# Weight sums of a seven-product matrix multiply, formed by accumulating DMAs in place of VectorE subtractions

## The chip, the core and the metric

The kernel runs on one NeuronCore of one Trainium2 chip. The core has five engines that each work through their own queue in order: TensorE (PE, with PEld for its weight loads), VectorE (DVE), ScalarE (ACT), GpSimd (POOL) and SyncE (SP, which here only issues DMAs). Data moves between the chip's main memory and the on-chip memory (128 partitions) by DMAs, which run on 16 DMA engines. The metric is the device time of one execution in microseconds; lower is better.

## The reference

One layer of a hybrid decoder on a sequence of 512 tokens with model width 2048. One large input projection feeds two branches, an mLSTM and a latent attention; their gated outputs are summed and projected back.

```
h = rms_norm(x, norm_g)                       # (512, 2048)
proj = h @ w_in                               # (2048, 15440), split into
(q_a, k_a, v_a, o_a, i_a, f_a, z_a, c_q, c_kv, k_r, z_b, g_a, g_b) = split(proj)
y_a = (sigmoid(o_a) * rms_norm(mlstm(q_a, k_a, v_a, ...)) * silu(z_a)) @ w_a
y_b = (attention(c_q, c_kv, k_r) * silu(z_b)) @ w_b
out = x + (sigmoid(g_a) * y_a + sigmoid(g_b) * y_b) @ w_out
```

Everything is float32. The five column blocks v_a, o_a, z_a, g_a and g_b of the projection, each 2048 columns wide, are where the change lies.

## The kernel before

TensorE multiplies in a rounded float32 format, so every operand is cut into a rounded high part and a remainder: `split` (L104) casts on ScalarE (L105) and subtracts on VectorE (L106), and each product takes three matmuls, high by high, high by low, low by high.

The five blocks are computed as ten jobs of 1024 columns (`strassen`, called for each of o, z, g_a, g_b, v twice). A job multiplies the 512 x 2048 input by a 2048 x 1024 weight block. Input and weights are cut into 2 x 2 quarters, and seven products of quarters take the place of eight. A weight quarter is 1024 rows by 512 columns; call them Q0 (top left), Q1 (top right), Q2 (bottom left), Q3 (bottom right). The seven passes p = 0 to 6 use these weights:

| pass | 0 | 1 | 2 | 3 | 4 | 5 | 6 |
|---|---|---|---|---|---|---|---|
| before | Q0 | Q1-Q0 | Q3-Q1+Q0 | Q3 | Q3-Q1 | Q2 | Q3-Q1+Q0-Q2 |

Each pass has four steps j, one for 256 rows of the quarter, so a job has 28 steps and the stage 280. In a step a tile of 128 partitions x 2 x 512 floats (512 KB) is split by `part` into `wh` (three buffers) and `wl` (two buffers), and `mult` runs 12 matmuls of 512 columns on it (L506 to L508). The program is written so that the split of step n+1 stands ahead of the matmuls of step n.

`prep` stands two steps ahead. It loads quarter tiles on SyncE's queue and forms the sums on VectorE (`minus`, L462). Per job and j it holds a tile x that starts as Q0 and is changed in place for passes 1, 2 and 6, and three tiles of a ring for Q1, Q3 and Q2; pass 4 changes the tile of Q3 in place. So a job has 16 loads of 512 KB and 16 subtractions. Outputs of passes are combined by `finish`, which puts small pieces of work on a list (`later`); one piece is taken per step. Results are stored by DMAs on ScalarE's queue, eight of 256 KB per job (16 for the two jobs of v).

The order in each engine's queue is set by the framework's scheduler from the program's order and from when buffers come free; it puts in the semaphore waits. GpSimd has no work between the input normalisation and the last steps of the stage. The program is built with `dynamic_dma_scratch_size=1024`, the bytes of each partition reserved for lists of DMAs that GpSimd's software issues; the kernel before issues none.

Of the kernel before, what the change touches and what calls it, by code (L numbers as in the profile page):

```python
# [11 lines left out]
F32 = mybir.dt.float32  # L12
# [4 lines left out]
ALU = mybir.AluOpType  # L17
AX = mybir.AxisListType

P = 128  # L20
# [14 lines left out]
OFF_C, OFF_ZB, OFF_GA, OFF_GB = 8208, 9296, 11344, 13392  # L35

NB_RAW, NB_W, NB_L, NB_A, NB_B, NB_HEAD, NB_T, NB_ACC, NB_AUX = 4, 3, 2, 15, 12, 17, 6, 5, 3
NB_X, NB_RING, NB_HI, NB_LO = 5, 8, 3, 2

KEYS_AHEAD, ATTN_STEP, MLSTM_STEP, OUT_AHEAD, RELOAD_STEP = 8000, 7800, 6000, 10000, 4000  # L40
EARLY = {"lat", "c", "gz", "vh", "vl", "rope", "rk"}
# [3 lines left out]
def hybrid_kernel(  # L45
# [8 lines left out]
    V, A, G, PE, SP = nc.vector, nc.scalar, nc.gpsimd, nc.tensor, nc.sync  # L54
# [21 lines left out]
    def nm(s):  # L76
        uid[0] += 1
        return f"{s}_{uid[0]}"
# [25 lines left out]
    def split(dst_hi, dst_lo, src):  # L104
        A.copy(dst_hi, src)  # L105
        V.tensor_tensor(dst_lo, src, f32(dst_hi), ALU.subtract)  # L106
# [39 lines left out]
    later = []  # L146
# [67 lines left out]
    H8 = KD // 2  # L214
# [70 lines left out]
    r = const([P, T], F32, "r")  # L285
# [14 lines left out]
    def build(j):  # L300
        f = whole[j]

        def normal():
            V.tensor_tensor(f, f, rB.unsqueeze(1).broadcast_to([P, 2, S]), ALU.mult)

        def parts():
            a = sap.tile([P, 2, 256], F32R, tag=f"a11_{j}", name=nm("a11"))
            b = tmp(512, "a21", F32R).rearrange("p (a c) -> p a c", a=2)
            for dst, n in ((a, 0), (b, 256)):
                split(dst[:, 0, :], dst[:, 1, :], f[:, 0, n:n + 256])  # L310
                SP.dma_start(htop_d[j][:, :, n:n + 256], f32(dst))
            hi = h8p.tile([P, S], F32R, tag=f"h8h{j}", name=nm("h8h"))
            lo = h8p.tile([P, S], F32R, tag=f"h8l{j}", name=nm("h8l"))
            split(hi, lo, f[:, 1, :])
            a11.append(a)
            hN[H8 + j] = (hi, lo)

        sums = []

        def combine():  # L320
            a, b = tmp(512, "s12"), tmp(512, "s34")
            s1, s2, s3, s4 = a[:, 0:256], a[:, 256:512], b[:, 0:256], b[:, 256:512]
            V.tensor_tensor(s1, f[:, 0, 256:512], f[:, 1, 256:512], ALU.add)
            V.tensor_tensor(s3, f[:, 0, 0:256], f[:, 0, 256:512], ALU.subtract)
            V.tensor_tensor(s2, s1, f[:, 0, 0:256], ALU.subtract)
            V.tensor_tensor(s4, f[:, 1, 0:256], s2, ALU.subtract)
            sums.extend((a, b))

        def split_sums():
            hi = sap.tile([P, 4, 256], F32R, tag=f"sh{j}", name=nm("sh"))  # L330
            lo = sap.tile([P, 4, 256], F32R, tag=f"sl{j}", name=nm("sl"))
            for n, src in enumerate(sums):
                src = src.rearrange("p (a c) -> p a c", a=2)
                split(hi[:, 2 * n:2 * n + 2, :], lo[:, 2 * n:2 * n + 2, :], src)
            sh.append(hi)
            sl.append(lo)

        return normal, parts, combine, split_sums
# [101 lines left out]
    def strassen(jobs, comb):  # L440

        count = [0]

        def load(src, row, col, ring):
            if ring:
                q = count[0] % NB_RING
                count[0] += 1
                raw = st["rra" if q < NB_RING - 1 else "rrb"].tile([P, 2, 512], F32, tag=f"rr{q}", name=nm("rr"))
            else:
                raw = st["rx"].tile([P, 2, 512], F32, tag="rx", name=nm("rx"), bufs=NB_X)  # L450
            SP.dma_start(raw, src[row:row + 256, col:col + 512].rearrange("(r p) c -> p r c", p=P))
            return raw

        half = H8 * P

        def prep(c, p, j):
            src, col = c["src"], c["col"]
            x, ring = c["x"], c["ring"]
            row = j * 256

            def minus(dst, a, b):
                V.tensor_tensor(dst, a, b, ALU.subtract)  # L462

            if p == 0:
                x[j] = load(src, row, col, False)
            elif p == 1:
                ring[0, j] = load(src, row, col + 512, True)
                minus(x[j], ring[0, j], x[j])
            elif p == 2:
                ring[1, j] = load(src, half + row, col + 512, True)  # L470
                minus(x[j], ring[1, j], x[j])
            elif p == 4:
                minus(ring[1, j], ring[1, j], ring[0, j])
            elif p == 5:
                ring[2, j] = load(src, half + row, col, True)
            elif p == 6:
                minus(x[j], x[j], ring[2, j])

        def part(c, p, j):
            w = c["ring"][1 if p in (3, 4) else 2, j] if p in (3, 4, 5) else c["x"][j]  # L480
            hi = st["wh"].tile([P, 2, 512], F32R, tag="sthi", name=nm("wh"), bufs=NB_HI)
            lo = st["wl"].tile([P, 2, 512], F32R, tag="stlo", name=nm("wl"), bufs=NB_LO)
            split(hi, lo, w)
            c["w"] = c.get("w", []) + [(hi, lo)]

        def mult(c, p, j):
            ps = c["ps"]
            if j == 0:
                if p == 0:
                    ps["a"] = [acc(), acc()]  # L490
                elif p == 1:
                    ps["c"] = [acc(), acc()]
                elif p in (2, 6):
                    ps["b"] = [aux(), aux()]
                elif p == 4:
                    ps["d"] = [acc(), aux()]
            out = ps["acbcdab"[p]]
            hi, lo = c["w"].pop(0)
            for n in range(2):
                k = 2 * j + n  # L500
                lh, ll = comb(p, k)
                for i in range(2):
                    tok = slice(i * P, (i + 1) * P)
                    first = k == 0 and p not in (3, 5)
                    cont = p in (3, 5)
                    PE.matmul(out[i], lh[:, tok], hi[:, n, :], start=first, stop=False, skip_group_check=cont)  # L506
                    PE.matmul(out[i], lh[:, tok], lo[:, n, :], start=False, stop=False, skip_group_check=cont)  # L507
                    PE.matmul(out[i], ll[:, tok], hi[:, n, :], start=False, stop=k == H8 - 1, skip_group_check=cont)  # L508

        def finish(c, p):  # L510
            ps, outs = c["ps"], c["outs"]

            def keep(name, src):
                c[name] = st["s15"].tile([P, 2, 512], F32, tag=name, name=nm(name))
                later.extend(lambda i=i: A.copy(c[name][:, i, :], src[i]) for i in range(2))

            def summed(i, t, n, a, b, op):
                o = tmp(512, "co")
                V.tensor_tensor(o, a, b, op)
                outs[n](t, o, True)  # L520

            if p == 0:
                keep("s1", ps["a"])
            elif p == 1:
                keep("s5", ps["c"])
            elif p in (2, 4):
                u, src = c["s1"], ps["b" if p == 2 else "d"]
                later.extend(lambda i=i: V.tensor_tensor(u[:, i, :], src[i], u[:, i, :], ALU.add) for i in range(2))
                if p == 4:
                    later.extend(lambda i=i: summed(i, 2 + i, 1, c["s5"][:, i, :], u[:, i, :], ALU.add) for i in range(2))  # L530
            elif p == 3:
                later.extend(lambda i=i: summed(i, i, 1, ps["c"][i], c["s1"][:, i, :], ALU.add) for i in range(2))
            elif p == 5:
                later.extend(lambda i=i: outs[0](i, ps["a"][i], False) for i in range(2))
            else:
                later.extend(lambda i=i: summed(i, 2 + i, 0, c["s1"][:, i, :], ps["b"][i], ALU.subtract) for i in range(2))

        steps = []
        for src, col, outs in jobs:
            c = dict(src=src, col=col, outs=outs, x={}, ring={}, ps={})  # L540
            steps += [(c, p, j) for p in range(7) for j in range(H8 // 2)]
        prep(*steps[0])
        prep(*steps[1])
        part(*steps[0])
        for n, s in enumerate(steps):
            if n + 2 < len(steps):
                prep(*steps[n + 2])
            if n + 1 < len(steps):
                part(*steps[n + 1])
            mult(*s)  # L550
            run_later()
            if s[2] == H8 // 2 - 1:
                finish(s[0], s[1])
            yield 12 * 512
# [13 lines left out]
    st = {n: open_pool(n, "right") for n in STP}  # L568
# [682 lines left out]
```

## Time and profile before

| | |
|---|---|
| median of 3 runs | 2174.47 us (2172.08 to 2177.78) |
| the profiled execution, its own time | 2176.62 us |
| its span, first to last instruction | 2174.9 us |
| busy: PE, DVE, ACT, POOL | 2121.5, 1395.4, 983.0, 173.2 us |
| granted TensorE clock, mean over the span | 0.991 |
| loads for the ten jobs | 160 of 512 KB, on SyncE's queue |

The profile is of one execution. PE's matmuls are pipelined: they overlap, so a matmul's own duration is longer than the distance to the next one. Rows by tile give the least, median and greatest duration in ns and the first and last start in us. In rows in order of time the bracket holds the idle time ahead and what ended it, in us. The seven-product stage runs from about 124 to about 880 us, at its end woven with the next stage.

### The profile page before, as it was taken

How to read it: one execution, taken by the hardware profiler on the slowest of the kernel's cores; microseconds unless marked ns; L12 is line 12 of the kernel's file. 1: busy time of each engine (PE TensorE's matmuls, PEld its weight loads, DVE VectorE, ACT ScalarE, POOL GpSimd, SP SyncE). 2: the span in 40 equal slices, each digit the busy share in tenths (PEclk: the TensorE clock that was granted, in tenths of full speed). 3: DMA queues.
4: the chain of work that ended last, by engine and by line, in shares of the span. 5: the costliest groups of instructions: out<-in, count | busy, mean ns of one | idle time of the engine just before them, and what ended most of it. 6: DMA issues, size and time to landing. Idle time of an engine off the chain costs nothing. (4 is left out here: it accounts for less than half of the span.)

```text
span 2174.9 us, 28907 instructions
## 1 busy us (share of the span) xinstructions
PE 2121.5 (98%) x10200; PEld 1787.8 (82%) x10200; DVE 1395.4 (64%) x2260; ACT 983.0 (45%) x2025; POOL 173.2 (8%) x306
## 2 busy tenths in 40 slices
PE   8999999999999999899999999999989999999999
PEld 8878888888888888688888888877867888888889
DVE  5877788887778788656666677766565334444333
ACT  7544444444444544445555556454445223222221
POOL 0000000000000000222222222011111000000000
PEclk9999999999999999999999999999999999999999
DMA  6645424633642462632222222464544425332443
GB/s 171 166 166 184 149 90 149 184 108 105 185 149 90 149 204 92 215 89 75 83 77 80 81 80 73 155 190 144 159 134 157 136 97 160 126 131 92 136 131 117
DMA packets 205314, 286.02 MB, mean 132 GB/s; under 512 B 31216, under 2 KB 111472, under 8 KB 204144
## 3 DMA queue, kind: packets, MB, share of 16 engines
q1 hardware_dynamic: 189040, 256.90, 38.9%
q10 hardware_dynamic: 16128, 27.27, 3.6%
q8 instruction: 80, 1.31, 0.3%
q14 instruction: 66, 0.54, 0.1%
HBM read 240.07 MB, written 44.04 MB: 131 GB/s over the span
## 5 line engine op out<-in xcount | busy, mean ns | idle before, releaser
L106 DVE TENSOR_TENSOR wlo<-raw,whi 128x512 fp32r<-128x512 f32 (+3 forms) x432 | 284.3, 661 | 383.5 <-PE acc L114 252.3
L105 ACT CAST whi<-raw 128x512 fp32r<-128x512 f32 (+3 forms) x432 | 259.1, 600 | 526.8 <-PE acc L115 338.0
L106 DVE TENSOR_TENSOR wl<-rx,wh 128x1024 fp32r<-128x1024 f32 x160 | 196.5, 1228 | 114.7 <-PE aux L507 64.7
L105 ACT CAST wh<-rx 128x1024 fp32r<-128x1024 f32 x160 | 168.9, 1055 | 177.9 <-PE acc L508 109.0
L113 PE MATMUL acc<-whi,g 128*128 128x512 f32 x512 | 201.5, 396 | 5.9 <-ACT g L105 5.9
L115 PE MATMUL acc<-whi,g 128*128 128x512 f32 x512 | 199.7, 393 | 1.8 <-DVE g L106 1.8
L114 PE MATMUL acc<-wlo,g 128*128 128x512 f32 x512 | 200.6, 392 | 0.0
L105 ACT CAST wh<-rr 128x1024 fp32r<-128x1024 f32 x120 | 126.4, 1053 | 160.7 <-PE aux L508 88.1
L106 DVE TENSOR_TENSOR wl<-rr,wh 128x1024 fp32r<-128x1024 f32 x120 | 146.3, 1219 | 27.6 <-PE aux L507 14.6
L506 PE MATMUL acc<-wh,sh 128*128 128x512 f32 x400 | 155.6, 389 | 0.0
L507 PE MATMUL acc<-wl,sh 128*128 128x512 f32 x400 | 155.6, 389 | 0.0
L508 PE MATMUL acc<-wh,sl 128*128 128x512 f32 x400 | 155.6, 389 | 0.0
L113 PEld LDWEIGHTS acc<-whi,g 128*128 128x128 f32 x512 | 96.8, 189 | 25.7 <-ACT g L105 6.5
L115 PEld LDWEIGHTS acc<-whi,g 128*128 128x128 f32 x512 | 96.9, 190 | 22.2 <-DVE g L106 2.2
L114 PEld LDWEIGHTS acc<-wlo,g 128*128 128x128 f32 x512 | 96.9, 189 | 20.3 <-DVE wlo L106 0.8
L115 PE MATMUL acc<-h8h,wlo 128*128 128x512 f32 x256 | 102.8, 406 | 10.3 <-DVE wlo L106 10.3
L113 PE MATMUL acc<-whi,y 128*128 128x512 f32 (+1 forms) x320 | 111.1, 348 | 0.0
L115 PE MATMUL acc<-whi,y 128*128 128x512 f32 (+1 forms) x320 | 111.0, 347 | 0.0
L114 PE MATMUL acc<-wlo,y 128*128 128x512 f32 (+1 forms) x320 | 111.0, 347 | 0.0
L113 PE MATMUL acc<-h8h,whi 128*128 128x512 f32 x256 | 103.6, 405 | 2.3 <-ACT whi L105 2.3
L114 PE MATMUL acc<-h8l,whi 128*128 128x512 f32 x256 | 102.5, 400 | 0.0
L113 PE MATMUL acc<-ht,whi 128*128 128x512 f32 x256 | 101.2, 395 | 0.0
(357 smaller groups left out, 5052.6 us busy)
## 6 DMA issues: line engine op xcount, KB each, us to landing
rr<-in_w_in SPq DMA_DIRECT2D x120, 512.0 KB, 4.6
raw<-in_w_in SPq DMA_DIRECT2D x128, 256.0 KB, 2.8
rx<-in_w_in SPq DMA_DIRECT2D x40, 512.0 KB, 5.0
raw<-in_w_b SPq DMA_DIRECT2D x64, 256.0 KB, 3.1
raw<-in_w_a SPq DMA_DIRECT2D x64, 256.0 KB, 3.2
raw<-in_w_out SPq DMA_DIRECT2D x64, 256.0 KB, 3.0
raw<-in_w_ukv SPq DMA_DIRECT2D x32, 256.0 KB, 2.8
raw<-in_w_uq SPq DMA_DIRECT2D x32, 192.0 KB, 2.4
```

The source lines that it names most:

```text
L105: A.copy(dst_hi, src)
L106: V.tensor_tensor(dst_lo, src, f32(dst_hi), ALU.subtract)
L113: PE.matmul(ps, lh, rh, start=start, stop=False)
L114: PE.matmul(ps, lh, rl, start=False, stop=False)
L115: PE.matmul(ps, ll, rh, start=False, stop=stop)
L506: PE.matmul(out[i], lh[:, tok], hi[:, n, :], start=first, stop=False, skip_group_check=cont)
L507: PE.matmul(out[i], lh[:, tok], lo[:, n, :], start=False, stop=False, skip_group_check=cont)
L508: PE.matmul(out[i], ll[:, tok], hi[:, n, :], start=False, stop=k == H8 - 1, skip_group_check=cont)
```

## The change

The signs of the quarters of the input are chosen anew so that every weight sum is an addition:

| pass | 0 | 1 | 2 | 3 | 4 | 5 | 6 |
|---|---|---|---|---|---|---|---|
| now | Q0 | Q0+Q1 | Q0+Q1+Q3 | Q3 | Q3+Q1 | Q2 | Q0+Q1+Q3+Q2 |

The sums are no longer formed on VectorE. Right behind the split of a tile, `grow` issues on GpSimd's queue a DMA that reads the next quarter from main memory and adds it to the tile where it lies. Tile x grows behind passes 0, 1 and 2 (by Q1, Q3, Q2), tile y (Q3) behind pass 3 (by Q1); z is Q2. Plain loads are 12 per job (x, y, z) and stand five steps ahead; all tiles come from one ring of 13. The input sums change signs (`combine`), and three output combinations swap addition and subtraction.

```
-NB_X, NB_RING, NB_HI, NB_LO = 5, 8, 3, 2
+NB_RING, NB_HI, NB_LO = 13, 3, 2
+LOAD_AHEAD = 5
...
-            V.tensor_tensor(s1, f[:, 0, 256:512], f[:, 1, 256:512], ALU.add)
+            V.tensor_tensor(s1, f[:, 0, 256:512], f[:, 1, 256:512], ALU.subtract)
...
-            V.tensor_tensor(s4, f[:, 1, 0:256], s2, ALU.subtract)
+            V.tensor_tensor(s4, f[:, 1, 0:256], s2, ALU.add)
...
+        def block(c, quarter, j):
+            row, col = j * 256 + (H8 * P if quarter >= 2 else 0), c["col"] + 512 * (quarter % 2)
+            return c["src"][row:row + 256, col:col + 512].rearrange("(r p) c -> p r c", p=P)
+
+        def load(c, p, j):
+
+            if p in (0, 3, 5):
                 q = count[0] % NB_RING
                 count[0] += 1
+                raw = st["rra" if q < 7 else "rx" if q < 12 else "rrb"].tile([P, 2, 512], F32, tag=f"rr{q}", name=nm("rr"))
+                c["xyz"[(0, 3, 5).index(p)], j] = raw
+                SP.dma_start(raw, block(c, {0: 0, 3: 3, 5: 2}[p], j))
...
-            if p == 0:
-                x[j] = load(src, row, col, False)
-            elif p == 1:
-                ring[0, j] = load(src, row, col + 512, True)
-                minus(x[j], ring[0, j], x[j])
-            elif p == 2:
-                ring[1, j] = load(src, half + row, col + 512, True)
-                minus(x[j], ring[1, j], x[j])
-            elif p == 4:
-                minus(ring[1, j], ring[1, j], ring[0, j])
-            elif p == 5:
-                ring[2, j] = load(src, half + row, col, True)
-            elif p == 6:
-                minus(x[j], x[j], ring[2, j])
+        def source(c, p, j):
+            return c["xxxyyzx"[p], j]
+
+        def grow(c, p, j):
+
+            quarter = {0: 1, 1: 3, 2: 2, 3: 1}.get(p)
+            if quarter is not None:
+                G.dma_start(source(c, p, j), block(c, quarter, j), accum_op=ALU.add)
 
         def part(c, p, j):
-            w = c["ring"][1 if p in (3, 4) else 2, j] if p in (3, 4, 5) else c["x"][j]
...
-            split(hi, lo, w)
+            split(hi, lo, source(c, p, j))
+            grow(c, p, j)
...
-            if n + 2 < len(steps):
-                prep(*steps[n + 2])
+            if n + LOAD_AHEAD < len(steps):
+                load(*steps[n + LOAD_AHEAD])
```

What this moves is seen in the engines' queues. First VectorE, in passes 3 and 4 of the first job; `wl` is the low part of a step, `rr` and `rx` are weight tiles, `s` and `co` outputs being combined. Before:

```order
L106 TENSOR_TENSOR wl_1855<-rr_1757,wh_1854 128x1024
L462 TENSOR_TENSOR rr_1757<-rr_1757,rr_1670 128x1024
L528 TENSOR_TENSOR s_330_1714<-aux_1803,s_330_1714 128x512
L106 TENSOR_TENSOR wl_1871<-rr_1776,wh_1870 128x1024
L528 TENSOR_TENSOR s_330_1714<-aux_1804,s_330_1714 128x512
L462 TENSOR_TENSOR rr_1776<-rr_1776,rr_1695 128x1024
L106 TENSOR_TENSOR wl_1888<-rr_1796,wh_1887 128x1024
L462 TENSOR_TENSOR rx_1606<-rx_1606,rr_1982 128x1024
L106 TENSOR_TENSOR wl_1906<-rr_1818,wh_1905 128x1024
```

Now:

```order
L107 TENSOR_TENSOR wl_1851<-rr_1769,wh_1850 128x1024
L516 TENSOR_TENSOR s_328_1713<-aux_1796,s_328_1713 128x512
L107 TENSOR_TENSOR wl_1868<-rr_1789,wh_1867 128x1024
L516 TENSOR_TENSOR s_328_1713<-aux_1797,s_328_1713 128x512
L107 TENSOR_TENSOR wl_1886<-rr_1811,wh_1885 128x1024
L107 TENSOR_TENSOR wl_1904<-rr_1831,wh_1903 128x1024
```

The subtractions of L462 are gone; splits and output sums are left in the same order.

GpSimd's queue, which is empty in this stage before, now holds passes 2 and 3 of the first job and pass 0 of the second as follows:

```order
L465 DMA rr_1606<-in_w_in 128x2x512
L465 DMA rr_1608<-in_w_in 128x2x512
L465 DMA rr_1610<-in_w_in 128x2x512
L465 DMA rr_1612<-in_w_in 128x2x512
L465 DMA rr_1769<-in_w_in 128x2x512
L465 DMA rr_1789<-in_w_in 128x2x512
L465 DMA rr_1811<-in_w_in 128x2x512
L465 DMA rr_1831<-in_w_in 128x2x512
L465 DMA rr_2072<-in_w_in 128x2x512
L465 DMA rr_2094<-in_w_in 128x2x512
L465 DMA rr_2117<-in_w_in 128x2x512
L465 DMA rr_2138<-in_w_in 128x2x512
```

The 16 accumulates of a job stand one behind the other, each waiting for its split, and nothing else stands between them.

SyncE's queue, from the first job's last plain load (its z tile rr_1984) to the second job's last x tile; in the second job x is 2072, 2094, 2117, 2138, y is 2307, 2327, 2349, 2369, z is 2458, 2476, 2500, 2522; 2610 is the third job's first x. Now:

```order
L456 DMA rr_1984<-in_w_in 128x2x512
L456 DMA rr_2072<-in_w_in 128x2x512
L456 DMA rr_2327<-in_w_in 128x2x512
L456 DMA rr_2349<-in_w_in 128x2x512
L456 DMA rr_2369<-in_w_in 128x2x512
L456 DMA rr_2458<-in_w_in 128x2x512
L456 DMA rr_2476<-in_w_in 128x2x512
L456 DMA rr_2500<-in_w_in 128x2x512
L456 DMA rr_2522<-in_w_in 128x2x512
L456 DMA rr_2610<-in_w_in 128x2x512
L456 DMA rr_2094<-in_w_in 128x2x512
L456 DMA rr_2117<-in_w_in 128x2x512
```

A tile of the ring is free when its old owner's last pass has been split, so y and z of the next job, which take the places of y and z of this one, are loaded ahead of the next job's x, in this job's passes 4 to 6.

More of the change, by code (lines that the diff above doesn't have):

```diff
@@ L442, in strassen @@
         count = [0]
-        def load(src, row, col, ring):
-            if ring:
+        def block(c, quarter, j):
[3 more added lines that the diff above has]
+            if p in (0, 3, 5):
                 q = count[0] % NB_RING
                 count[0] += 1
[L448 to L462, printed above, removed]
-            if p == 0:
-                x[j] = load(src, row, col, False)
-            elif p == 1:
-                ring[0, j] = load(src, row, col + 512, True)
-                minus(x[j], ring[0, j], x[j])
-            elif p == 2:
-                ring[1, j] = load(src, half + row, col + 512, True)
-                minus(x[j], ring[1, j], x[j])
-            elif p == 4:
-                minus(ring[1, j], ring[1, j], ring[0, j])
-            elif p == 5:
-                ring[2, j] = load(src, half + row, col, True)
-            elif p == 6:
-                minus(x[j], x[j], ring[2, j])
+                raw = st["rra" if q < 7 else "rx" if q < 12 else "rrb"].tile([P, 2, 512], F32, tag=f"rr{q}", name=nm("rr"))
@@ L529, in finish @@
                 if p == 4:
-                    later.extend(lambda i=i: summed(i, 2 + i, 1, c["s5"][:, i, :], u[:, i, :], ALU.add) for i in range(2))
+                    later.extend(lambda i=i: summed(i, 2 + i, 1, c["s5"][:, i, :], u[:, i, :], ALU.subtract) for i in range(2))
             elif p == 3:
-                later.extend(lambda i=i: summed(i, i, 1, ps["c"][i], c["s1"][:, i, :], ALU.add) for i in range(2))
+                later.extend(lambda i=i: summed(i, i, 1, ps["c"][i], c["s1"][:, i, :], ALU.subtract) for i in range(2))
             elif p == 5:
@@ L535, in finish @@
             else:
-                later.extend(lambda i=i: summed(i, 2 + i, 0, c["s1"][:, i, :], ps["b"][i], ALU.subtract) for i in range(2))
+                later.extend(lambda i=i: summed(i, 2 + i, 0, c["s1"][:, i, :], ps["b"][i], ALU.add) for i in range(2))
         steps = []
         for src, col, outs in jobs:
-            c = dict(src=src, col=col, outs=outs, x={}, ring={}, ps={})
+            c = dict(src=src, col=col, outs=outs, ps={})
             steps += [(c, p, j) for p in range(7) for j in range(H8 // 2)]
-        prep(*steps[0])
-        prep(*steps[1])
+        for s in steps[:LOAD_AHEAD]:
+            load(*s)
         part(*steps[0])
         for n, s in enumerate(steps):
-            if n + 2 < len(steps):
-                prep(*steps[n + 2])
+            if n + LOAD_AHEAD < len(steps):
+                load(*steps[n + LOAD_AHEAD])
             if n + 1 < len(steps):
```

## The prediction

> **What bounds the kernel now.** I began with the page's first part, to see which engine fills the span, and with the time of the stage that the change touches.
>
> ```profile
> span 2174.9 us, 28907 instructions
> PE 2121.5 (98%) x10200; PEld 1787.8 (82%) x10200; DVE 1395.4 (64%) x2260; ACT 983.0 (45%) x2025; POOL 173.2 (8%) x306
> 138.30:870.00 731.70, 731.70 (x3229) 605.86 (x3228) 578.13 (x556) 346.31 (x383) 0.00 (x0) 1.00 0.45 138
> ```
>
> The third line is a row of the table by stretches: stretch, length, busy time of PE, PEld, DVE, ACT and POOL, granted clock, mean share of the DMA engines, GB/s. In nearly the whole seven-product stage TensorE is busy for 731.70 of 731.70 us at full clock, VectorE for 79%, GpSimd not at all. Next the list of waits, for PE, from 120 to 870 us, says what TensorE ever waits for there:
>
> ```profile
> PE acc L506 <- ACT wh L105: 2.8, 1, 2.8
> PE acc L507 <- DVE wl L106: 0.5, 1, 0.5
> ```
>
> That is 3.3 us in all, at the stage's very start. So VectorE's work here, however large, holds nobody up. The transfers of SyncE's queue give the rhythm:
>
> ```profile
> 236.30 29.04 SPq L451 DMA_DIRECT2D rr<-in_w_in  x12
> 312.46 29.01 SPq L451 DMA_DIRECT2D rr<-in_w_in  x12
> ```
>
> One job (28 steps: seven products of four steps) takes 312.46 - 236.30 = 76.16 us, one step 2.72 us of matmuls without a gap.
>
> **What is removed, at no gain.** The view of the tile rr gives the removed subtractions and the work that stays:
>
> ```profile
> L105 ACT CAST wh<-rr x120: 1029/1056/1059, 155.1 to 870.6; 128x1024 fp32r<-128x1024 f32 x120
> L462 DVE TENSOR_TENSOR rx<-rr,rx x80: 1215/1224/1227, 131.9 to 830.7; 128x1024 f32<-128x1024 f32 x80
> L462 DVE TENSOR_TENSOR rr<-rr,rr x40: 1211/1219/1227, 158.9 to 853.5; 128x1024 f32<-128x1024 f32 x40
> L462 DVE TENSOR_TENSOR rx<-rx,rr x40: 1211/1217/1221, 164.6 to 863.3; 128x1024 f32<-128x1024 f32 x40
> DMA to landing us min/median/max: 3.5/4.6/10.5
> ```
>
> 160 subtractions of 1.22 us are 195 us of VectorE, all beside a TensorE that never waits for them: worth 0. SyncE issues 120 loads in place of 160; its queue is not what ends anything, worth 0. The sign changes in `combine`, `summed` and the last output swap add for subtract in the same instructions: 0. The scheduler also moves the y and z loads of the next job ahead into passes 4 to 6, behind the last accumulate; they need 12 x 1.72 = 21 us of engine time (1.72 us is worked out below) in 12 steps = 33 us, so I take 0 there too.
>
> **What is added.** 160 accumulating DMAs of 512 KB on GpSimd's queue, 16 per job, one behind each split of passes 0 to 3. Each has to wait for VectorE's split, because it overwrites what the split reads, and the split of the same tile one pass later has to wait until it has landed. When must it land to be hidden? The order of time on VectorE and TensorE:
>
> ```profile
> 228.35 1.22 DVE L106 TENSOR_TENSOR wl<-rx,wh 128x1024 fp32r<-128x1024 f32 x1 [1.48 <-PE aux L507]
> 231.04 0.39 PE L506 MATMUL aux<-wh,sh 128*128 128x512 f32 x1
> ```
>
> The split for the step that starts at 231.04 ends at 229.57, that is 1.47 us ahead of its matmuls. The same tile's next step starts four steps later, at 231.04 + 10.88 = 241.92, and its cast (1.06) and split (1.22) have to lie before that: the accumulate must land by 239.64, 10.07 us after it could be issued. One landing of 3.5 to 4.6 us fits twice over. So latency alone costs nothing; what counts is T, the time from one accumulate's landing to the next one's.
>
> The rate matters because the 16 come in one row. From the first accumulate's issue to the last one's landing takes 16 T. Then come cast and split (2.28), the nine steps 19 to 27 (24.48), and the next job's first accumulate may go 1.47 before its step 0. A job cannot be shorter than
>
> 16 T + 2.28 + 24.48 - 1.47 = 16 T + 25.29 us.
>
> It stays at 76.16 as long as T is at most (76.16 - 25.29) / 16 = 3.18 us. Beyond that each job loses 16 (T - 3.18), ten times over.
>
> No accumulate and no transfer from GpSimd's queue is in the trace, so I bound T. Rows for the speed of the 16 engines when full, and the one for loads in a job:
>
> ```profile
> 350.00:355.00 5.00, 5.00 (x23) 4.13 (x23) 2.72 (x3) 2.11 (x2) 0.00 (x0) 1.00 1.00 305
> 130.00:135.00 5.00, 5.00 (x23) 4.08 (x22) 4.70 (x7) 2.11 (x2) 0.00 (x0) 0.96 1.05 391
> rr<-in_w_in SPq DMA_DIRECT2D x120, 512.0 KB, 4.6
> ```
>
> 524,288 bytes take 1.34 us at 391 GB/s and 1.72 us at 305. From below: an accumulate costs the engines one plain pass and many are in flight, T = 1.34, nothing lost. From above: they run one at a time, each with the median landing of a load (4.6) and one more pass over 512 KB for the old sum, which has to be read as well (1.72): T = 6.32, a job of 126.4, +50.3 each, +503 in all.
>
> I take one at a time, with the shortest landing seen (3.5, a queue with little else on it; in passes 0 to 3 SyncE's loads are now mostly out of the way) and the second pass at the fast row: T = 3.5 + 1.34 = 4.84. The reason for one at a time lies in the program, not in the trace: its last lines reserve only 1,024 bytes of each partition for the lists that a software-issued DMA is written into (dynamic_dma_scratch_size), and a DMA of 256 rows spread over 16 engines needs a list of 16 rows on each, for the new numbers and again for the old ones. SyncE's queue does overlap its loads (one every 2.72 us with 4.6 us to landing), which speaks for the other side.
>
> The Trainium skill bears on this in two pages: "DMA: Bandwidth & Descriptors" (Terms; The descriptor swizzle) has 16 bytes for a descriptor and, for a software-issued transfer over 128 partitions, one completion descriptor per side and engine beside the data; "Collectives: The Full Stack" (The bandwidth ceiling: the fold count) has two read descriptors per piece for an add, on one ring. By these an accumulate takes 2 x 16 + 1 = 33 of 1,024 / 16 = 64 places, so that a second does not fit, and the forecast holds; were it 17, three would fit and nothing would be lost. No run here shows it yet. The first page's fit for software-issued DMAs (Anatomy of one DMA) gives 2.0 + 524,288 / 436,000 = 3.2 us where the trace has 3.5 to 4.6 for SyncE's; an estimate by it, with 1.2 more for the second read, is T = 4.4 and a time of 2372.
>
> **The sum.** Job: 16 x 4.84 + 25.29 = 102.73, against 76.16: +26.57, ten jobs +266 us. The profiled execution took 2176.6 us (span 2174.9), so 2176.6 + 266 = 2442. The median of the runs shown is 2174.5, 2 us less, which is nothing here.
>
> One thing is left out of the sum and kept in the range. TensorE would now stand still in passes 1 to 4, longest before pass 4: step 15 ends 54.6 us after the job's first issue, the 13th accumulate lands at 62.9 and its split is done at 65.2, a gap of 10.6. The trace shows what a gap does:
>
> ```profile
> 124.21 1.22 PE L506 MATMUL acc<-wh,a 128*128 128x512 f32 x2 [2.77 <-ACT wh L105]
> 129.50 0.63 PE L507 MATMUL acc<-wl,a 128*128 128x512 f32 x1
> 125.00:130.00 5.00, 4.51 (x12) 3.21 (x11) 4.22 (x9) 2.87 (x5) 0.00 (x0) 0.50 0.99 324
> 902.40 0.51 PE L507 MATMUL aux<-wl,h8h 128*128 128x512 f32 x1 [1.90 <-DVE wl L106]
> ```
>
> After 2.77 us idle the granted clock was 0.50 for the next 5 us or more, matmuls 0.43 apart instead of 0.227; after 1.90 us idle they ran on at full pace. A step at half clock takes 12 x 0.43 = 5.1 us, hardly more than T, so the loss is the last such step and little more, 0 to 3 us per job, up to 30 in all.
>
> **The rivals.**
> 1. *The engines set the pace.* Several accumulates are in flight, and each costs two passes at the slow row: 3.44, and four 256 KB stores in the same time add 1.05 MB / 305 GB/s / 16 = 0.21: T = 3.65, job 83.7, +75, time 2252. At the fast row T is 2.85 and nothing is lost. For it: loads overlap on SyncE's queue. Against: the small reserve.
> 2. *It is hidden.* T at most 3.18; the change then takes work off VectorE, which was waited for by nobody, and the time stays at 2177. For it: the 10.07 us of room for each landing, and a DMA share of only 0.45. Against: the same, as under 1, if old and new numbers both pass the engines.
> 3. *Faster.* VectorE, relieved, removes the waits of TensorE around the stage. The wait at 124.21 comes ahead of the first subtraction (131.9), so it stays. The rows behind the stage:
>
> ```profile
> 800.00:900.00 100.00, 95.52 (x410) 77.38 (x409) 79.90 (x120) 49.42 (x74) 13.07 (x24) 0.98 0.44 136
> 900.00:1000.00 100.00, 98.10 (x500) 83.09 (x499) 61.67 (x135) 50.41 (x149) 16.99 (x20) 1.00 0.42 133
> 865.00:870.00 5.00, 4.18 (x6) 1.00 0.96 247
> 870.00:875.00 5.00, 4.71 (x12) 1.00 0.95 300
> ```
>
> TensorE is idle for 4.5 + 1.9 us there, and VectorE already has pauses at 865 to 875 (the last two rows are of VectorE alone: stretch, busy time, clock, DMA share, GB/s), after the last subtraction (863.3) and ahead of the wait at 902.40; so a backlog of subtractions is not what makes it late. With all 9.7 us gone (3.3 + 4.5 + 1.9) the time would be 2167.
> 4. *Longer still.* GpSimd's own work on each DMA comes on top of the landing, or landings are above the median: T over 6.32, time over 2679.
>
> **How the numbers follow.** Chances: one at a time, 2442, 0.50 (its own range 2228 to 2679: T = 3.5, a bare shortest landing, gives a job of 81.3 and +51; T = 6.32 gives +503); engines set the pace, 2252, 0.16; hidden, 2177, 0.23; faster, 2167, 0.04; longer still 0.07. A measurement of this kernel tells 0.3%, about 6.5 us, from no change. Slower: 0.50 + 0.16 + 0.07 = 0.73; within 0.3%: 0.23; faster: 0.04. For 8 in 10 the range has to take in the hidden case, since the slower cases below 2679 hold only 0.66: from 2170 (a few us under hidden) to 2680, with 0.11 left out. The cases of both signs are not in balance; the likeliest one's own range is the one above.
>
> **What would show it.** In the changed kernel's profile:
> - VectorE busy about 1200 us (1395 - 195), 160 DMA issues on GpSimd's queue of 512 KB each; their spacing within a job's row of 16 is T itself. At 2.7 (one per step) the hidden case is right, near 3.6 with the DMA share near 1.0 the engines, at 4.8 with a DMA share well below 1.0 the forecast.
> - SyncE's or GpSimd's rows come back after T's value: 102.7 us per job instead of 76.16.
> - TensorE waits for wh and wl whose own releaser is a DMA on rr, with one gap of about 10 us per job ahead of pass 4 and gaps of about 2 us in pass 2 and pass 4; granted clock 0.5 behind the long one. Passes 5 and 6 run without a gap.
> - Outside 120 to 880 us of the old order of time nothing changes its length.
> The prediction is wrong if accumulates overlap on GpSimd's queue (landing longer than their spacing), or if T stays under 3.18.

## The result

The change made the kernel slower: 2671.85 us median (2669.87 to 2678.8) against 2173.97 us, a ratio of 1.2293 with a 95% interval of 1.2264 to 1.2322. That is 498 us more, or 49.8 us for each of the ten jobs. The forecast was 2442 us, in a range from 2170 to 2680.

The page of the changed kernel, its span and busy times, the row of GpSimd's queue among the DMA queues (packets, MB, share of the 16 engines), and the two issues that matter (KB each, median us to landing):

```profile
span 2671.8 us, 29163 instructions
PE 2279.5 (85%) x10200; PEld 1849.6 (69%) x10200; DVE 1216.0 (46%) x2100; ACT 975.7 (37%) x2025; POOL 368.8 (14%) x466
q0 software_dynamic: 43520, 83.90, 20.3%
rr<-in_w_in POOLq DMA_DIRECT2D x160, 512.0 KB, 5.8
rr<-in_w_in SPq DMA_DIRECT2D x120, 512.0 KB, 5.1
```

VectorE lost 179 us of work, near the 195 forecast, and nobody gained by it: TensorE went from 98% of the span to 85%. Where its time went is in the list of waits (engine, line, what it waited for; us in all, times, longest):

```profile
ACT wh L106 <- DMA rr<-in_w_in: 661.1, 105, 22.7
PE acc L494 <- ACT wh L106: 216.8, 53, 16.7
PE aux L494 <- ACT wh L106: 55.1, 32, 2.8
PE acc L495 <- DVE wl L107: 46.1, 61, 2.5
PE aux L495 <- DVE wl L107: 30.2, 43, 2.5
```

TensorE waits for the cast, and the cast for a DMA into the weight tile. That DMA is an accumulate: the view of its line, L465, names the same casts as what waited for it, 661.1 us in 105 times. GpSimd's own order of time (start, length, and in the bracket the idle time ahead and what ended it) shows how they follow one another:

```profile
255.73 1.21 POOL L465 DMA_DIRECT2D rr<-in_w_in  x1 [30.39 <-DVE wl L107]
...
342.21 1.21 POOL L465 DMA_DIRECT2D rr<-in_w_in  x1 [4.83 <-issue]
348.28 1.21 POOL L465 DMA_DIRECT2D rr<-in_w_in  x1 [4.86 <-issue]
379.94 1.21 POOL L465 DMA_DIRECT2D rr<-in_w_in  x1 [30.45 <-DVE wl L107]
386.17 1.20 POOL L465 DMA_DIRECT2D rr<-in_w_in  x1 [5.01 <-issue]
```

From 255.73 to 348.28 the 16 accumulates of one job are issued, 92.55 / 15 = 6.17 us apart. The landing takes 5.8 us from issue (first fence). By the issue and landing times in the trace, none of the 160 is issued before the one ahead of it has landed, and most go 0.32 us after that. Over the whole run, GpSimd's pauses ahead of an accumulate (us in all, times) mostly end on this:

```profile
  issue: 690.3, 138
```

"issue" means that no semaphore seen by the profile held GpSimd. One job goes from 255.73 to 379.94, 124.2 us.

TensorE's order of time in this job:

```profile
281.24 0.50 PE L494 MATMUL acc<-wh,sh 128*128 128x512 f32 x1 [2.07 <-ACT wh L106]
337.03 0.79 PE L494 MATMUL acc<-wh,sh 128*128 128x512 f32 x1 [15.67 <-ACT wh L106]
```

Stretches of it, the row of 16 accumulates first (length, then busy time and instructions of PE, PEld, DVE, ACT, POOL, granted clock, DMA share, GB/s):

```profile
255.73:348.28 92.55, 61.21 (x222) 44.93 (x220) 24.33 (x23) 19.90 (x23) 18.26 (x15) 0.85 0.59 102
285.00:290.00 5.00, 4.54 (x14) 2.96 (x13) 1.23 (x1) 1.04 (x1) 1.22 (x1) 0.63 0.43 60
290.00:295.00 5.00, 2.10 (x9) 1.18 (x8) 1.22 (x1) 1.53 (x2) 1.21 (x1) 1.00 0.43 71
295.00:300.00 5.00, 4.43 (x12) 3.02 (x12) 0.24 (x1) 1.31 (x2) 1.10 (x1) 0.66 0.60 98
335.00:340.00 5.00, 2.50 (x5) 1.71 (x6) 1.82 (x2) 1.04 (x1) 1.22 (x1) 0.50 0.42 59
360.00:365.00 5.00, 5.00 (x24) 4.14 (x23) 3.78 (x6) 2.72 (x5) 0.00 (x0) 1.00 0.81 239
```

There is one long gap per job ahead of pass 4 (15.67 us), gaps of about 2 us in the passes before and after it, and the passes 5 and 6 run without a pause at full clock. While the accumulates go one at a time, the 16 engines are not full: a share of 0.59 over the row.

### The profile page after: what moved, and what is told of

The parts are those of the page before. It is cut to its first block, busy times and chain, and to the rows that moved or that the text cites. A ratio compares the mean times of both kernels' runs of the same rounds, so it can differ in the third digit from the quotient of the medians.

```text
span 2671.8 us, 29163 instructions
## 1 busy us (share of the span) xinstructions
PE 2279.5 (85%) x10200; PEld 1849.6 (69%) x10200; DVE 1216.0 (46%) x2100; ACT 975.7 (37%) x2025; POOL 368.8 (14%) x466
## 3 DMA queue, kind: packets, MB, share of 16 engines
q0 software_dynamic: 43520, 83.90, 20.3%
## 5 line engine op out<-in xcount | busy, mean ns | idle before, releaser
L107 DVE TENSOR_TENSOR wl<-rr,wh 128x1024 fp32r<-128x1024 f32 x280 | 341.9, 1227 | 766.4 <-ACT wh L106 637.7
L106 ACT CAST wh<-rr 128x1024 fp32r<-128x1024 f32 x280 | 290.2, 1049 | 870.0 <-DMA rr<-in_w_in 661.1
L465 POOL DMA_DIRECT2D rr<-in_w_in x160 | 194.9, 1218 | 1099.1 <-issue 690.3
L494 PEld LDWEIGHTS acc<-wh,sh 128*128 128x128 f32 x400 | 85.3, 213 | 257.6 <-ACT wh L106 240.5
L494 PE MATMUL aux<-wh,sh 128*128 128x512 f32 x240 | 119.7, 499 | 55.1 <-ACT wh L106 55.1
L495 PEld LDWEIGHTS acc<-wl,sh 128*128 128x128 f32 x400 | 85.6, 214 | 84.8 <-DVE wl L107 68.2
L495 PE MATMUL aux<-wl,sh 128*128 128x512 f32 x240 | 119.8, 499 | 26.3 <-DVE wl L107 26.3
L494 PEld LDWEIGHTS aux<-wh,sh 128*128 128x128 f32 x240 | 57.7, 240 | 86.6 <-ACT wh L106 73.7
L496 PE MATMUL aux<-wh,sl 128*128 128x512 f32 x240 | 114.3, 476 | 0.0
L114 PE MATMUL acc<-whi,y 128*128 128x512 f32 (+1 forms) x320 | 111.1, 348 | 0.0
```

What stands on the lines that cost most here:

```text
L114: PE.matmul(ps, lh, rh, start=start, stop=False)
L465: G.dma_start(source(c, p, j), block(c, quarter, j), accum_op=ALU.add)
```

## The experiments

Two theories stood against each other. Theory 1: the 1,024 bytes reserved per partition hold the list of one accumulate only, so the next is not written before the last has landed. Theory 2: an accumulate of 512 KB simply takes 6 us, in the engines or in GpSimd's software. Four kernels ran together first, beside the kernel before (2175.65 us median in these runs).

### More room for the lists

```
-NB_RING, NB_HI, NB_LO = 13, 3, 2
+NB_RING, NB_HI, NB_LO = 12, 3, 2
...
-    nc = _bacc.Bacc(..., dynamic_dma_scratch_size=1024)
+    nc = _bacc.Bacc(..., dynamic_dma_scratch_size=2048)
```

> The change with 2,048 in place of 1,024 bytes per partition reserved for software-issued DMAs; to make room, the ring of tiles goes from 13 to 12. Theory 1 (the reserve lets only one accumulate be under way): two or more are under way now, the spacing on GpSimd's queue falls from 6.2 us to the steps' own 2.7, or to 3.65 if the engines then set the pace; a job takes 76.2 to 84 us in place of 125; time 2172 to 2255 us. Theory 2 (an accumulate of 512 KB takes the engines or GpSimd's software about 6 us each, however many may wait): spacing stays at 6.2, time stays at about 2670.

Measured: 2181.93 us, ratio to the kernel before 1.0032 (1.0018 to 1.0045). Nearly the whole loss is gone. GpSimd's order of time in one job, then its pauses over the whole run (us, times), the stretch of that job, and its queue's share in two jobs:

```profile
362.40 1.20 POOL L465 DMA_DIRECT2D rr<-in_w_in  x1 [34.15 <-DVE wl L107]
365.21 1.20 POOL L465 DMA_DIRECT2D rr<-in_w_in  x1 [1.61 <-DVE wl L107]
...
376.56 1.20 POOL L465 DMA_DIRECT2D rr<-in_w_in  x1 [2.08 <-DMA rr<-in_w_in]
...
400.48 1.22 POOL L465 DMA_DIRECT2D rr<-in_w_in  x1 [1.43 <-DVE wl L107]
403.20 1.21 POOL L465 DMA_DIRECT2D rr<-in_w_in  x1 [1.50 <-DVE wl L107]
```
```profile
  DVE wl L107: 427.6, 92
  DMA rr<-in_w_in: 93.3, 56
  issue: 6.4, 4
```
```profile
362.40:438.56 76.16, 76.16 (x338) 63.07 (x337) 45.00 (x46) 35.89 (x40) 19.36 (x16) 1.00 0.99 221
```
```profile
q0 software_dynamic: 8704, 16.78, 62.5%
rr<-in_w_in POOLq DMA_DIRECT2D x33, 512.0 KB, 7.3
```

Accumulates now go 2.72 us apart, (403.20 - 362.40) / 15. The pauses on "issue" are all but gone, 4 in place of 138: 92 of GpSimd's pauses end on VectorE's split, and 56 still on the landing of an earlier accumulate. They land after 7.3 us, and by issue and landing times three are under way at 138 of the 160 issues, and never more. So GpSimd can still wait for a landing, but for that of the accumulate three places ahead, which comes soon enough. The job takes 76.16 us to the hundredth, TensorE does not wait in it, and the 16 engines are full (0.99). In 153 us the packets of the queue took 62.5% of the engines' time for 32 accumulates (16.78 MB): 2.99 us of all 16 engines for each. Theory 1 holds, theory 2 falls.

### The smaller ring of tiles alone

```
-NB_RING, NB_HI, NB_LO = 13, 3, 2
+NB_RING, NB_HI, NB_LO = 12, 3, 2
```

> The change with the ring of tiles at 12 in place of 13 and the reserve as it was, 1,024 bytes. Both theories: nothing moves, about 2672 us; a next job's first x tile is then loaded behind step 24 of this one, 11 us before it is needed, against a landing of about 5 us.

Measured: 2652.33 us in one run, 20 us (0.7%) under the change, which was not expected and stays unexplained; the accumulates' landing is 5.7 us. The ring's size is not what brought the 490 us.

### Half an accumulate at a time

```
-G.dma_start(source(c, p, j), block(c, quarter, j), accum_op=ALU.add)
+for r in range(2):
+    G.dma_start(source(c, p, j)[:, r:r + 1, :], block(c, quarter, j)[:, r:r + 1, :], accum_op=ALU.add)
```

> The change with each accumulate issued as two of 256 KB (one per row of 128 partitions), reserve 1,024 bytes. Theory 1: half an accumulate needs half the places, so three halves are under way at once; 512 KB then take two thirds of a landing of 5 to 5.8 us, 3.4 to 3.9 us, or twice GpSimd's own 1.21 us where that is more; a job takes 79 to 88 us, time 2210 to 2290. Theory 2, engines: the same bytes take the same 6 us, time about 2670. Theory 2, GpSimd's software: the number of DMAs doubles, time above 2670.

Measured: 2306.57 us in one run, where theory 1 had 2210 to 2290. With the same small reserve and the same bytes, 365 us of the loss are gone; the forecast was 17 us too low at its slow end. By issue and landing times three halves are under way from the third of a job on, never more, and 259 pauses still end on "issue", 246.8 us in all. The row by source line (least, median, greatest ns of one):

```profile
L466 POOL DMA_DIRECT2D rr<-in_w_in x320: 856/865/1243, 123.6 to 985.0; - x160
```

GpSimd's instruction lasts 0.87 us for a half, in all more than for whole ones, and the kernel is still far faster: the time that GpSimd's software needs to write a DMA is not what sets the pace.

### The same DMAs as plain copies

```
-G.dma_start(source(c, p, j), block(c, quarter, j), accum_op=ALU.add)
+G.dma_start(source(c, p, j), block(c, quarter, j))
```

> The change with the 160 DMAs on GpSimd's queue as plain copies: nothing is added, so all weight sums are only the last quarter loaded; same tiles, same waits, same bytes from main memory, reserve 1,024 bytes. Theory 1: a copy needs about half the places of an accumulate, three are under way, spacing 2.7 us, time 2170 to 2185. If the slow part is the add in the engines: also about 2175. If it is GpSimd's software, which would let one DMA land before it writes the next: spacing 4.5 to 5.8 us, time 2400 to 2610.

Measured: 2174.81 us in one run, no different from the kernel before. The rows by source line, two of GpSimd's order of time, and the queue's share in the same stretch of 153 us as above:

```profile
L465 POOL DMA_DIRECT2D rr<-in_w_in x160: 722/722/951, 124.9 to 852.0; - x160
DMA to landing us min/median/max: 3.6/4.9/8.4
```
```profile
367.83 0.72 POOL L465 DMA_DIRECT2D rr<-in_w_in  x1 [1.99 <-DVE wl L107]
370.55 0.72 POOL L465 DMA_DIRECT2D rr<-in_w_in  x1 [2.00 <-DVE wl L107]
```
```profile
q0 software_dynamic: 4651, 16.96, 36.2%
```

Plain copies from GpSimd's queue do overlap in the same 1,024 bytes: they go 2.72 us apart and land after 4.9. This run alone does not part theory 1 from a slow add in the engines; the other kernels do. A copy costs GpSimd 0.72 us and the engines 36.2% x 153 / 32.3 = 1.71 us, an accumulate at 2,048 bytes 1.21 us and 2.99 us: 1.7 times the engine time for the same bytes from main memory. In the changed kernel itself the page gives 20.3% x 2671.8 / 160 = 3.39 us for an accumulate, twice the copy, so this is what the packets took in each run and no fixed price.

Four more kernels ran together (before: 2173.13 us median).

### Rows or bytes

Halves again, this time cut by columns, so that each half has all 256 rows at half the length.

```
-G.dma_start(source(c, p, j), block(c, quarter, j), accum_op=ALU.add)
+for r in range(2):
+    w = slice(256 * r, 256 * r + 256)
+    G.dma_start(source(c, p, j)[:, :, w], block(c, quarter, j)[:, :, w], accum_op=ALU.add)
```

> The change, reserve 1,024 bytes, with each accumulate issued as two of 256 KB that are cut by columns: all 256 rows, each of 1 KB. Theory of places (a row takes places in the list, whatever its length): each of the two still fills the list alone, so they go one at a time, 4.9 to 5.4 us each, 10 to 10.8 us for 512 KB; job 16 x 10.3 + 25.3 = 190 us, time 3200 to 3400. Theory of bytes (so many KB may be under way): as with the halves cut by rows, about 2307 us.

Measured: 3217.5 us in one run. The rows by source line and a piece of GpSimd's order of time:

```profile
L467 POOL DMA_DIRECT2D rr<-in_w_in x320: 1203/1213/1415, 126.3 to 1895.3; - x160
DMA to landing us min/median/max: 4.1/4.4/8.1
```
```profile
605.36 1.21 POOL L467 DMA_DIRECT2D rr<-in_w_in  x1 [3.69 <-issue]
610.00 1.22 POOL L467 DMA_DIRECT2D rr<-in_w_in  x1 [3.43 <-issue]
614.78 1.21 POOL L467 DMA_DIRECT2D rr<-in_w_in  x1 [3.55 <-issue]
```

One at a time again, (614.78 - 605.36) / 2 = 4.71 us apart, with GpSimd's full 1.21 us for each. Of two kernels with the same 320 DMAs of 256 KB, the one with 128 rows each took 2307 us, the one with 256 rows 3218 us. What fills the reserve is rows, not bytes; and since plain copies of 256 rows overlap in it, rows of an accumulate fill more of it than rows of a copy.

### One tile fewer in the row

```
-quarter = {0: 1, 1: 3, 2: 2, 3: 1}.get(p)
+quarter = {0: 1, 1: 3, 2: 2}.get(p)
```

> The change, reserve 1,024 bytes, without the four accumulates behind pass 3 of each job (160 become 120): pass 4 then multiplies Q3 in place of Q3+Q1, so part of each job's product is left out. Theory of the row (PE waits for the chain of accumulates, each 6.17 us behind the one before): pass 2's last step now follows the eighth accumulate, and nothing later in the job waits for one in time: 8 x 6.17 + 2.28 + 17 x 2.72 - 1.47 = 96.4 us per job, +202, time 2375 to 2395. If each accumulate cost its excess over the step wherever it stands: 120/160 of the 497 us lost, time 2547.

Measured: 2383.72 us in one run, inside the 2375 to 2395 of the row's theory and far from the 2547 that a price per accumulate would give. From the second job on, jobs start 94.9 to 100.2 us apart by GpSimd's first accumulate of each; 96.4 was worked out.

### What is left over at 2,048 bytes

The kernel with 2,048 bytes still lost 0.3%. Its jobs begin, by GpSimd's first accumulate of each, at 128.98, 210.08, 286.24, 362.40 us: the first takes 81.1, every other one 76.16. So 4.9 us are lost in the first job alone. Two kernels try to get them back: halves cut by rows at 2,048 bytes (twice the bytes written ahead), and the first job's loads of y and z held back.

```
...
+if c["job"] == 0 and p > 0:
+    V.tensor_copy(raw[:, 0, 0:1], f32(c["w"][-1][1][:, 0, 0:1]))
...
```

> Reserve 2,048 bytes, ring of 12, each accumulate as two halves cut by rows, so that twice as many bytes may be written ahead. If what is left over before (2182 against 2175.7) comes from the number that may be under way: 2172 to 2177 us. If it comes from the engines being full in the first job: 2178 to 2187 us.

> Reserve 2,048 bytes, ring of 12, and in the first job alone the eight plain loads of y and z are held back (a one-column copy from the split five steps ahead is written into the tile first), so that they no longer run beside the first accumulates. If the 4.9 us that the first job takes longer than the others come from these loads taking the engines from the accumulates: the first job falls to 76 to 78 us and the time to 2176 to 2180 us. If not, it stays at 2182.

Measured: 2180.34 us (1.0027, 1.0016 to 1.0039) and 2180.82 us (1.0033, 1.0023 to 1.0044). Neither helps, and the first job takes 81.55 and 81.1 us, though with halves up to seven DMAs are under way at once. Two stretches of the first job, first of the kernel with 2,048 bytes:

```profile
140.00:150.00 10.00, 7.79 (x31) 5.11 (x29) 3.67 (x3) 3.41 (x5) 3.07 (x3) 1.00 1.10 262
170.00:180.00 10.00, 10.00 (x46) 8.28 (x45) 5.66 (x6) 3.32 (x4) 3.51 (x3) 1.00 1.13 204
```

And of the one with held loads:

```profile
140.00:150.00 10.00, 10.00 (x45) 8.29 (x45) 5.05 (x6) 4.66 (x5) 4.47 (x4) 1.00 1.08 210
170.00:180.00 10.00, 8.23 (x33) 5.58 (x32) 5.24 (x8) 4.31 (x5) 1.22 (x1) 1.00 1.10 260
```

Holding the loads moved TensorE's pauses, which lay between 141 and 154 us, to between 170 and 184 us and left their size, about 3 us in all. In all four stretches the engines are full (1.08 to 1.13), which fits with the first job having more to carry than they can, in whatever order; with plain copies, which cost the engines less, the first job took 76.96. That the engines are the cause is thus argued and not shown; shown is only that neither the number under way nor these eight loads' early start is. No version here beats the kernel before: from the second job on its 76.16 us per job are TensorE's own, and at 2,048 bytes the changed kernel has the same 76.16.

## Why the prediction was right or wrong

**The removed work** was rightly priced at 0. The kernels with 2,048 bytes and with plain copies have VectorE relieved in the same way, and neither is faster than before.

**The mechanism** was right: accumulates one at a time, chained to TensorE by the 16-long row, with T as the only number that counts. The reason given, the small reserve, is shown by the 2,048 bytes and by the two ways of halving at 1,024. The formula for a job, 16 T + 25.29, gives 124.0 us with the measured T = 6.17; the ten jobs' mean is 76.16 + 49.8 = 126.0, of which the first alone took 131.5. The kernel without the pass 3 accumulates confirms it from the other side.

**The step that fell short** is a term of the sum: T = 3.5 + 1.34 = 4.84 us measured 6.17. With the formula the 1.33 us are 16 x 1.33 x 10 = 213 of the 230 us missed. Both parts were too small. For 3.5, the shortest landing of a load on SyncE's queue, a plain copy from GpSimd's queue takes 3.6 at least, so that part was nearly right; but from landing to the next issue go another 0.32, which the sum did not have. For 1.34, the second pass over the bytes at the fastest row of the trace, accumulates take 5.7 at least, 2.1 more than plain copies: GpSimd's instruction lasts 1.21 in place of 0.72 us, and 1.6 are left, nearer the slow row's 1.72. That these 1.6 are the second pass is argued and not shown: by the pages of the two kernels an accumulate also has 43520 / 160 = 272 packets where a plain copy has 23040 / 160 = 144, and no run parts the two. GpSimd's own writing time was missing from the sum, although it was named under the fourth rival.

**The range** took the result in by 8 us, and some luck is in that. Its upper end, T = 6.32, was the median landing, 4.6, and the slow pass, 1.72; it too had neither GpSimd's longer instruction nor the 0.32, and a landing 1 us longer than the shortest copy's stood in for them.

**The Trainium skill's pages** that the prediction names, "DMA: Bandwidth & Descriptors" (Terms; The descriptor swizzle) and "Collectives: The Full Stack" (The bandwidth ceiling: the fold count), put together, gave an estimate of 33 of 64 places for an accumulate; the same count gives 17 for a half of 128 rows and 17 for a plain copy. Then 1,024 bytes hold one whole accumulate, three halves by rows or three copies, and 2,048 bytes three whole ones or seven halves, and these are the greatest numbers under way in the six kernels (table at the end). That goes further than one against several, but the count is still not shown: 32 and 16 places with one kept free would give the same. The estimate by the first page's fit (Anatomy of one DMA), T = 4.4, was further off than the rows.

**The rivals.** That the engines set the pace was priced at T = 3.65 and does not happen: with room for the lists they are at 0.99 and just keep up, with 2.99 us of their time for an accumulate where 3.44 was assumed. So with 2,048 bytes the same change is the hidden case, but for the first job.

**The clock.** Half clock was expected behind the long gap and not behind gaps of 2 us, since one of 1.90 us before did nothing. It came behind the long gap (0.50 from 335 to 340 us), but also in places behind the gaps of about 2 us: 0.63, 1.00 and 0.66 in the three stretches from 285 to 300 us, 0.85 over the whole row. It costs little, as said, because a step at half clock (5.1 us) fits between two landings 6.17 apart; what is left of the miss, 17 of 230 us, includes it.

## What to carry to other kernels

Moving work off an engine that nobody waits for cannot gain, but it can put a new chain on the path: count how many links it has in a row, and compare the time per link with the time that hides one. A software-issued DMA needs room for its list, by rows; in the 1,024 bytes of a program that had issued no such DMA, one accumulate at a time fits, and doubling the reserve, by 1 KB of each partition, was worth 490 us. An accumulate took the engine time of 1.7 to 2 plain copies here, and may fill the engines even where latency is hidden.

## What the runs showed of the hardware

- How many DMAs of GpSimd's queue were under way at once, at most, by their issue and landing times:

| DMAs | reserve, bytes | most under way |
|---|---|---|
| accumulates, 256 rows of 2 KB | 1,024 | 1 |
| accumulates, 256 rows of 1 KB | 1,024 | 1 |
| accumulates, 128 rows of 2 KB | 1,024 | 3 |
| plain copies, 256 rows of 2 KB | 1,024 | 3 |
| accumulates, 256 rows of 2 KB | 2,048 | 3 |
| accumulates, 128 rows of 2 KB | 2,048 | 7 |

  In the first three GpSimd pauses on "issue" 138, 305 and 259 times, so there the reserve is the limit; in the others it does so 1, 4 and 2 times, so they show only that as many fit.
- A full reserve shows in the trace as pauses of GpSimd on "issue", with the next DMA about 0.3 us after a landing.
- At 1,024 bytes GpSimd's instruction for one DMA lasts 0.72 us for a copy of 256 rows, 0.87 for an accumulate of 128 rows, 1.21 for one of 256 rows, whether a row has 1 KB or 2 KB. At 2,048 bytes the halves of 128 rows took 0.85 to 1.32, median 1.02, so rows and kind do not fix it alone.
- One at a time, an accumulate of 256 rows takes 4.71 us with rows of 1 KB and 6.17 with rows of 2 KB, so 256 KB more add 1.46 us.
- With gaps of about 2 us repeated every 6 us TensorE's granted clock went down and up again: 0.63, 1.00 and 0.66 in stretches of 5 us, 0.85 over 92.55 us. A single gap of 1.90 us had left it at 1.00.
